# RMSNorm with GELU in fp32: tiles of two rows per partition, statistics in pairs, Gelu in place, and a fixed order of VectorE and ScalarE

## Chip, cores, metric

One core of a Trainium2 chip. The metric is the device time of one execution in us. A kernel's executions spread by at most 0.3%.

## The reference

```python
x: (8, 1024, 2048) float32, gamma: (2048,) float32, eps = 1e-5
rms = np.sqrt(np.mean(x ** 2, axis=-1, keepdims=True) + eps)
out = gamma * x / rms
return 0.5 * out * (1 + np.tanh(np.sqrt(2 / np.pi) * (out + 0.044715 * out ** 3)))
```

8192 rows of 2048 numbers: 67.1 MB in, 67.1 MB out.

## The kernel before

64 tiles of 128 rows. Loads are issued by SyncE, stores by GpSimd. ScalarE squares x with the sum as a by-product (and later does Gelu with the row's factor as its scale); VectorE multiplies by gamma and computes 1/sqrt of the mean square with an integer trick and two Newton steps, nine instructions on one column. A scheduler places the instructions of each engine.

```python
xpool bufs=8; ypool bufs=5; opool bufs=8; spool bufs=12; psum bufs=2
gamma_t = singles.tile([P, D], fp32)
nc.sync.dma_start(out=gamma_t, in_=gamma.partition_broadcast(P))
for i in range(ntiles):                       # 64
    x_t = xpool.tile([P, D], fp32)
    nc.sync.dma_start(out=x_t, in_=x2d[r0:r0 + P, :])
    nc.scalar.activation(out=sq_scratch, in_=x_t, func=Square, scale=inv_d_sqrt, accum_out=ssq)
    y_t = ypool.tile([P, D], fp32)
    nc.vector.tensor_mul(out=y_t, in0=x_t, in1=gamma_t)
    # ... nine VectorE instructions on [P, 1]: rstd from ssq (cut)
    o_t = opool.tile([P, D], fp32)
    nc.scalar.activation(out=o_t, in_=y_t, func=Gelu_apprx_tanh, scale=rstd)
    nc.gpsimd.dma_start(out=out2d[r0:r0 + P, :], in_=o_t)
```

Of the kernel before, what the change touches and what calls it, by code (L numbers as in the profile page):

```python
# [1 line left out]

# [4 lines left out]


@with_exitstack  # L10
def kernel(
    ctx: ExitStack,
    tc: tile.TileContext,
    x: bass.AP,
    gamma: bass.AP,
    eps: bass.AP,
    out: bass.AP,
):
    nc = tc.nc
    P = nc.NUM_PARTITIONS  # L20
    fp32 = mybir.dt.float32

    x2d = x.flatten_outer_dims()
    out2d = out.flatten_outer_dims()
    N, D = x2d.shape
    assert N % P == 0
    ntiles = N // P

    eps_f = float(eps)
    inv_d_sqrt = 1.0 / float(D) ** 0.5  # L30

    MAGIC = 0x5F3759DF

    singles = ctx.enter_context(tc.tile_pool(name="singles", bufs=1))
    xpool = ctx.enter_context(tc.tile_pool(name="xpool", bufs=8))
    ypool = ctx.enter_context(tc.tile_pool(name="ypool", bufs=5))
    opool = ctx.enter_context(tc.tile_pool(name="opool", bufs=8))
    spool = ctx.enter_context(tc.tile_pool(name="spool", bufs=12))
    psum = ctx.enter_context(tc.tile_pool(name="psum", bufs=2, space=bass.MemoryType.PSUM))

    gamma_t = singles.tile([P, D], fp32)
    nc.sync.dma_start(out=gamma_t, in_=gamma.partition_broadcast(P))

    magic_t = singles.tile([P, 1], mybir.dt.int32)
    nc.vector.memset(magic_t, MAGIC)  # L45

    for i in range(ntiles):
        r0 = i * P

        x_t = xpool.tile([P, D], fp32)  # L50
        nc.sync.dma_start(out=x_t, in_=x2d[r0:r0 + P, :])  # L51

        sq_scratch = psum.tile([P, D], fp32)
        stats = spool.tile([P, 8], fp32)
        ssq = stats[:, 0:1]
        nc.scalar.activation(  # L56
            out=sq_scratch,
            in_=x_t,
            func=mybir.ActivationFunctionType.Square,
            scale=inv_d_sqrt,  # L60
            accum_out=ssq,
        )

        y_t = ypool.tile([P, D], fp32)
        nc.vector.tensor_mul(out=y_t, in0=x_t, in1=gamma_t)  # L65

        a = stats[:, 1:2]
        g0 = stats[:, 2:3]
        t0 = stats[:, 3:4]
        t1 = stats[:, 4:5]  # L70
        rstd = stats[:, 5:6]

        nc.vector.tensor_single_scalar(out=a, in_=ssq, scalar=eps_f, op=mybir.AluOpType.add)  # L73
        a_i = a.bitcast(mybir.dt.int32)
        g0_i = g0.bitcast(mybir.dt.int32)
        t0_i = t0.bitcast(mybir.dt.int32)
        nc.vector.tensor_single_scalar(out=t0_i, in_=a_i, scalar=1, op=mybir.AluOpType.arith_shift_right)  # L77
        nc.vector.tensor_tensor(out=g0_i, in0=magic_t, in1=t0_i, op=mybir.AluOpType.subtract)  # L78

        nc.vector.scalar_tensor_tensor(  # L80
            out=t0, in0=g0, scalar=g0, in1=a,
            op0=mybir.AluOpType.mult, op1=mybir.AluOpType.mult,
        )
        nc.vector.tensor_scalar(  # L84
            out=t1, in0=t0, scalar1=-0.5, scalar2=1.5,
            op0=mybir.AluOpType.mult, op1=mybir.AluOpType.add,
        )
        nc.vector.tensor_mul(out=g0, in0=g0, in1=t1)  # L88

        nc.vector.scalar_tensor_tensor(  # L90
            out=t0, in0=g0, scalar=g0, in1=a,
            op0=mybir.AluOpType.mult, op1=mybir.AluOpType.mult,
        )
        nc.vector.tensor_scalar(  # L94
            out=t1, in0=t0, scalar1=-0.5, scalar2=1.5,
            op0=mybir.AluOpType.mult, op1=mybir.AluOpType.add,
        )
        nc.vector.tensor_mul(out=rstd, in0=g0, in1=t1)  # L98

        o_t = opool.tile([P, D], fp32)  # L100
        nc.scalar.activation(  # L101
            out=o_t,
            in_=y_t,
            func=mybir.ActivationFunctionType.Gelu_apprx_tanh,
            scale=rstd,
        )

        nc.gpsimd.dma_start(out=out2d[r0:r0 + P, :], in_=o_t)  # L108


# [1 line left out]
_INS = ['x', 'gamma', 'eps']  # L112
_OUTS = [((8, 1024, 2048), 'float32')]
#: Inputs that are plain numbers.
_NUMBERS = {'eps': 9.999999747378752e-06}


# [26 lines left out]
```

## Time and profile before

| | before |
|---|---|
| time, median of 13 runs | 331.67 us (331.3 to 332.27) |
| span of the profiled run | 330.0 us |
| bytes moved by DMA | 135.35 MB, 410 GB/s over the span |
| VectorE, ScalarE busy | 225.4 us (68%), 247.4 us (75%) |

A page of the profile shows the span in 40 slices of equal length: the busy tenths of each engine, the mean busy share of the 16 DMA engines, and the GB/s that they moved. Here the last two rows say nearly all: from the fourth slice to the 36th the engines' share stands at 9 tenths and the rate at 423 to 429 GB/s, while VectorE is busy for 68% of the span and ScalarE for 75%; in the first three slices and the last four it is lower in places, and there lie the 13.2 us of the span that 135.27 MB at 427 GB/s do not explain. The prediction shows those rows and the windows at both ends. The page lists the packets of one queue as "instruction" (packets, MB, share of the 16 engines' time); they are called fetches below:

```profile
q14 instruction: 9, 0.07, 0.1%
```

### The profile page before, as it was taken

The numbers are of one execution on the slowest core, as the hardware profiler recorded it, in microseconds if no ns is written. First come the engines' busy times: TensorE is split into PE (matmuls) and PEld (weight loads), VectorE is DVE, ScalarE is ACT, GpSimd is POOL, SyncE is SP. The second block draws the span as 40 slices with busy tenths as digits, with TensorE's granted clock in tenths as the row PEclk, the third lists the DMA queues.
The fourth block names the chain that finished last, engine by engine and source line by source line (L and its number), as shares of the span: only waits on it lengthen the run. The fifth ranks groups of instructions, "written<-read, shape, count | busy, mean of one in ns | idle before, by whom it ended". The sixth has DMA issues, their size and how long they took to land.

```text
span 330.0 us, 1300 instructions
## 1 busy us (share of the span) xinstructions
DVE 225.4 (68%) x641; ACT 247.4 (75%) x194; POOL 34.4 (10%) x68
## 2 busy tenths in 40 slices
DVE  0998747647676775958686775949686775869630
ACT  2899794937695969687686969686786969596990
POOL 0020100201010101011010101011010101011110
DMA  8999999999999999999999999999999999999765
GB/s 319 419 382 423 426 426 428 428 428 427 428 427 428 427 426 426 427 429 425 428 427 428 428 427 428 425 426 427 428 427 426 428 427 428 429 427 387 313 286 207
DMA packets 18585, 135.35 MB, mean 410 GB/s; under 512 B 2064, under 2 KB 2064, under 8 KB 2064
## 3 DMA queue, kind: packets, MB, share of 16 engines
q1 hardware_dynamic: 9360, 68.16, 49.2%
q0 software_dynamic: 9216, 67.11, 48.3%
q14 instruction: 9, 0.07, 0.1%
HBM read 68.16 MB, written 67.11 MB: 410 GB/s over the span
## 4 chain that ended last, share of the span: by engine, by line
issue 40%; DMA 40%; ACT 7%; DVE 5%; POOL 5%; POOLq 0%; SPq 0%; ACTq 0%; DVEq 0%
DMA x_t<-in_x_dram 40%; POOL out_dram L108 5%; ACT sq_scratch L56 5%; DVE y_t L65 3%; ACT o_t L101 2%; DVE stats L80 0%; DVE stats L78 0%; DVE stats L77 0%; DVE stats L84 0%; DVE stats L90 0%; POOLq L139 0%; DVE stats L88 0%; DVE stats L73 0%; POOLq L108 0%; SPq L51 0%
## 5 line engine op out<-in xcount | busy, mean ns | idle before, releaser
L65 DVE TENSOR_TENSOR y_t<-x_t,gamma_t 128x2048 f32<-128x2048 f32 x64 | 146.6, 2292 | 76.6 <-DMA x_t<-in_x_dram 73.7
L101 ACT ACTIVATE o_t<-y_t,stats 128x2048 f32<-128x2048 f32 x64 | 123.6, 1991 | 66.2 <-DVE stats L98 66.2
L56 ACT ACTIVATE sq_scratch<-x_t 128x2048 f32<-128x2048 f32 x64 | 119.0, 1859 | 7.0 <-DMA x_t<-in_x_dram 7.0
L108 POOL DMA_DIRECT2D out_dram<-o_t x64 | 34.2, 535 | 287.5 <-ACT o_t L101 287.5
L90 DVE SCALAR_TENSOR_TENSOR stats<-stats 128x1 f32<-128x1 f32 x64 | 13.9, 219 | 1.4
L80 DVE SCALAR_TENSOR_TENSOR stats<-stats 128x1 f32<-128x1 f32 x64 | 13.7, 217 | 1.3
L73 DVE TENSOR_SCALAR stats<-stats 128x1 f32<-128x1 f32 x64 | 9.2, 147 | 5.1 <-ACT sq_scratch L56 5.1
L56 ACT ACTIVATION_READ_ACCUMULATOR sq_scratch<-x_t 128x1 f32 x64 | 11.9, 186 | 0.0
L88 DVE TENSOR_TENSOR stats<-stats 128x1 f32<-128x1 f32 x64 | 10.1, 159 | 1.8
L98 DVE TENSOR_TENSOR stats<-stats 128x1 f32<-128x1 f32 x64 | 10.1, 159 | 1.3
L84 DVE TENSOR_SCALAR stats<-stats 128x1 f32<-128x1 f32 x64 | 9.7, 153 | 1.7
L78 DVE TENSOR_TENSOR stats<-magic_t,stats 128x1 int32<-128x1 int32 x64 | 9.9, 157 | 1.3
L94 DVE TENSOR_SCALAR stats<-stats 128x1 f32<-128x1 f32 x64 | 9.8, 153 | 1.3
L77 DVE TENSOR_SCALAR stats<-stats 128x1 int32<-128x1 int32 x64 | 9.5, 151 | 1.3
L56 ACT ACT_TABLE_LOAD x1 | 1.3, 1283 | 0.7 <-PEq L125 0.7
L101 ACT ACT_TABLE_LOAD x1 | 1.3, 1283 | 0.0
L45 DVE MEMSET magic_t<- 128x1 int32 x1 | 0.1, 59 | 0.8 <-PEq L125 0.8
L125 POOL MEMSET const-float32-0.0<- 128x1 f32 x1 | 0.1, 100 | 0.2 <-issue 0.2
L125 POOL MEMSET const-bfloat16-1.0<- 128x1 bf16 x1 | 0.1, 103 | 0.0
L125 POOL MEMSET const-float32-1.0<- 128x1 f32 x1 | 0.1, 100 | 0.0
L125 POOL MEMSET const-uint8-127<- 128x1 uint8 x1 | 0.1, 100 | 0.0
## 6 DMA issues: line engine op xcount, KB each, us to landing
x_t<-in_x_dram SPq DMA_DIRECT2D x64, 1024.0 KB, 26.2
out_dram<-o_t POOLq DMA_DIRECT2D x64, 1024.0 KB, 12.8
gamma_t<-in_gamma_dram SPq DMA_DIRECT2D x1, 1024.0 KB, 4.5
```

The costliest lines, as they stand in the source:

```text
L56: nc.scalar.activation(out=sq_scratch, in_=x_t, func=mybir.ActivationFunctionType.Square, scale=inv_d_sqrt, accum_out=ssq,)
L65: nc.vector.tensor_mul(out=y_t, in0=x_t, in1=gamma_t)
L77: nc.vector.tensor_single_scalar(out=t0_i, in_=a_i, scalar=1, op=mybir.AluOpType.arith_shift_right)
L78: nc.vector.tensor_tensor(out=g0_i, in0=magic_t, in1=t0_i, op=mybir.AluOpType.subtract)
L80: nc.vector.scalar_tensor_tensor(out=t0, in0=g0, scalar=g0, in1=a, op0=mybir.AluOpType.mult, op1=mybir.AluOpType.mult,)
L84: nc.vector.tensor_scalar(out=t1, in0=t0, scalar1=-0.5, scalar2=1.5, op0=mybir.AluOpType.mult, op1=mybir.AluOpType.add,)
L88: nc.vector.tensor_mul(out=g0, in0=g0, in1=t1)
L90: nc.vector.scalar_tensor_tensor(out=t0, in0=g0, scalar=g0, in1=a, op0=mybir.AluOpType.mult, op1=mybir.AluOpType.mult,)
L94: nc.vector.tensor_scalar(out=t1, in0=t0, scalar1=-0.5, scalar2=1.5, op0=mybir.AluOpType.mult, op1=mybir.AluOpType.add,)
L98: nc.vector.tensor_mul(out=rstd, in0=g0, in1=t1)
L101: nc.scalar.activation(out=o_t, in_=y_t, func=mybir.ActivationFunctionType.Gelu_apprx_tanh, scale=rstd,)
L108: nc.gpsimd.dma_start(out=out2d[r0:r0 + P, :], in_=o_t)
```

## The change

Its intent: fewer and larger transfers with longer contiguous runs, fewer small VectorE instructions, one tile less in SBUF, and an order of the two engines that is fixed by hand.

```diff
+    R = 2                                  # rows per partition in a tile: 32 tiles of 256 rows
+    x3d = x2d.rearrange("(n p r) d -> n p r d", p=P, r=R)
+    o3d = out2d.rearrange("(n p r) d -> n p r d", p=P, r=R)
-    xpool bufs=8, ypool bufs=5, opool bufs=8
+    xpool bufs=5, ypool bufs=5
+    def front(i):
+        x_t = xpool.tile([P, R, D], fp32);  nc.sync.dma_start(out=x_t, in_=x3d[i])
+        for r in range(R):  # Square of x_t[:, r, :], sum to ms[:, r:r + 1]
+        # ... eleven VectorE instructions on [P, R] in place of 2 x nine on [P, 1] (cut)
+        nc.vector.tensor_mul(out=y_t, in0=x_t, in1=gamma_b)       # after the statistics
+        return y_t, g
+    def back(i, y_t, g):
+        for r in range(R):  # Gelu of y_t[:, r, :] in place, scale=g[:, r:r + 1]
+        nc.gpsimd.dma_start(out=o3d[i], in_=y_t)
+    with tc.manual_schedule(engines={DVE, Activation}):
+        prev = front(0)
+        for i in range(1, ntiles):
+            cur = front(i);  back(i - 1, *prev);  prev = cur
+        back(ntiles - 1, *prev)
```

More of the change, by code (lines that the diff above doesn't have):

```diff
@@ L21 @@
     fp32 = mybir.dt.float32
+    int32 = mybir.dt.int32
     x2d = x.flatten_outer_dims()
@@ L25 @@
     N, D = x2d.shape
-    assert N % P == 0
-    ntiles = N // P
+    R = 2
+    rows_per_tile = P * R
+    assert N % rows_per_tile == 0
+    ntiles = N // rows_per_tile
     eps_f = float(eps)
@@ L32 @@
     MAGIC = 0x5F3759DF
+    x3d = x2d.rearrange("(n p r) d -> n p r d", p=P, r=R)
+    o3d = out2d.rearrange("(n p r) d -> n p r d", p=P, r=R)
     singles = ctx.enter_context(tc.tile_pool(name="singles", bufs=1))
-    xpool = ctx.enter_context(tc.tile_pool(name="xpool", bufs=8))
+    xpool = ctx.enter_context(tc.tile_pool(name="xpool", bufs=5))
     ypool = ctx.enter_context(tc.tile_pool(name="ypool", bufs=5))
-    opool = ctx.enter_context(tc.tile_pool(name="opool", bufs=8))
     spool = ctx.enter_context(tc.tile_pool(name="spool", bufs=12))
@@ L39 @@
     psum = ctx.enter_context(tc.tile_pool(name="psum", bufs=2, space=bass.MemoryType.PSUM))
-    gamma_t = singles.tile([P, D], fp32)
+    gamma_t = singles.tile([P, 1, D], fp32)
     nc.sync.dma_start(out=gamma_t, in_=gamma.partition_broadcast(P))
-    magic_t = singles.tile([P, 1], mybir.dt.int32)
+    gamma_b = gamma_t.to_broadcast([P, R, D])
+    magic_t = singles.tile([P, R], int32)
     nc.vector.memset(magic_t, MAGIC)
-    for i in range(ntiles):
-        r0 = i * P
-        x_t = xpool.tile([P, D], fp32)
-        nc.sync.dma_start(out=x_t, in_=x2d[r0:r0 + P, :])
-        sq_scratch = psum.tile([P, D], fp32)
-        stats = spool.tile([P, 8], fp32)
-        ssq = stats[:, 0:1]
-        nc.scalar.activation(
-            out=sq_scratch,
-            in_=x_t,
-            func=mybir.ActivationFunctionType.Square,
-            scale=inv_d_sqrt,
-            accum_out=ssq,
-        )
-        y_t = ypool.tile([P, D], fp32)
-        nc.vector.tensor_mul(out=y_t, in0=x_t, in1=gamma_t)
-        a = stats[:, 1:2]
-        g0 = stats[:, 2:3]
-        t0 = stats[:, 3:4]
-        t1 = stats[:, 4:5]
-        rstd = stats[:, 5:6]
-        nc.vector.tensor_single_scalar(out=a, in_=ssq, scalar=eps_f, op=mybir.AluOpType.add)
-        a_i = a.bitcast(mybir.dt.int32)
-        g0_i = g0.bitcast(mybir.dt.int32)
-        t0_i = t0.bitcast(mybir.dt.int32)
-        nc.vector.tensor_single_scalar(out=t0_i, in_=a_i, scalar=1, op=mybir.AluOpType.arith_shift_right)
-        nc.vector.tensor_tensor(out=g0_i, in0=magic_t, in1=t0_i, op=mybir.AluOpType.subtract)
-        nc.vector.scalar_tensor_tensor(
-            out=t0, in0=g0, scalar=g0, in1=a,
-            op0=mybir.AluOpType.mult, op1=mybir.AluOpType.mult,
-        )
-        nc.vector.tensor_scalar(
-            out=t1, in0=t0, scalar1=-0.5, scalar2=1.5,
-            op0=mybir.AluOpType.mult, op1=mybir.AluOpType.add,
-        )
-        nc.vector.tensor_mul(out=g0, in0=g0, in1=t1)
-        nc.vector.scalar_tensor_tensor(
-            out=t0, in0=g0, scalar=g0, in1=a,
-            op0=mybir.AluOpType.mult, op1=mybir.AluOpType.mult,
-        )
-        nc.vector.tensor_scalar(
-            out=t1, in0=t0, scalar1=-0.5, scalar2=1.5,
-            op0=mybir.AluOpType.mult, op1=mybir.AluOpType.add,
-        )
-        nc.vector.tensor_mul(out=rstd, in0=g0, in1=t1)
-        o_t = opool.tile([P, D], fp32)
-        nc.scalar.activation(
-            out=o_t,
-            in_=y_t,
-            func=mybir.ActivationFunctionType.Gelu_apprx_tanh,
-            scale=rstd,
-        )
-        nc.gpsimd.dma_start(out=out2d[r0:r0 + P, :], in_=o_t)
@@ new lines, in front @@
+    def front(i):
+        x_t = xpool.tile([P, R, D], fp32, name="x_t")
+        nc.sync.dma_start(out=x_t, in_=x3d[i])
+        sq_scratch = psum.tile([P, D], fp32, name="sq_scratch")
+        stats = spool.tile([P, 4, R], fp32, name="stats")
+        ms = stats[:, 0, :]
+        for r in range(R):
+            nc.scalar.activation(
+                out=sq_scratch,
+                in_=x_t[:, r, :],
+                func=mybir.ActivationFunctionType.Square,
+                scale=inv_d_sqrt,
+                accum_out=ms[:, r:r + 1],
+            )
+        a = stats[:, 1, :]
+        g = stats[:, 2, :]
+        t = stats[:, 3, :]
+        nc.vector.tensor_single_scalar(out=a, in_=ms, scalar=eps_f, op=mybir.AluOpType.add)
+        nc.vector.tensor_single_scalar(
+            out=t.bitcast(int32), in_=a.bitcast(int32), scalar=1,
+            op=mybir.AluOpType.arith_shift_right,
+        )
+        nc.vector.tensor_tensor(
+            out=g.bitcast(int32), in0=magic_t, in1=t.bitcast(int32),
+            op=mybir.AluOpType.subtract,
+        )
+        for _ in range(2):
+            nc.vector.tensor_mul(out=t, in0=g, in1=g)
+            nc.vector.tensor_mul(out=t, in0=t, in1=a)
+            nc.vector.tensor_scalar(
+                out=t, in0=t, scalar1=-0.5, scalar2=1.5,
+                op0=mybir.AluOpType.mult, op1=mybir.AluOpType.add,
+            )
+            nc.vector.tensor_mul(out=g, in0=g, in1=t)
+        y_t = ypool.tile([P, R, D], fp32, name="y_t")
+        nc.vector.tensor_mul(out=y_t, in0=x_t, in1=gamma_b)
+        return y_t, g
@@ new lines, in back @@
+    def back(i, y_t, g):
+        for r in range(R):
+            nc.scalar.activation(
+                out=y_t[:, r, :],
+                in_=y_t[:, r, :],
+                func=mybir.ActivationFunctionType.Gelu_apprx_tanh,
+                scale=g[:, r:r + 1],
+            )
+        nc.gpsimd.dma_start(out=o3d[i], in_=y_t)
+    with tc.manual_schedule(engines={mybir.EngineType.DVE, mybir.EngineType.Activation}):
+        prev = front(0)
+        for i in range(1, ntiles):
+            cur = front(i)
+            back(i - 1, *prev)
+            prev = cur
+        back(ntiles - 1, *prev)
```

## The prediction

> **What bounds the kernel now.** I read the page first, from the slices down. The first fence has the busy tenths and the DMA rows of the page before.
>
> ```profile
> DVE  0998747647676775958686775949686775869630
> ACT  2899794937695969687686969686786969596990
> ...
> DMA  8999999999999999999999999999999999999765
> GB/s 319 419 382 423 426 426 428 428 428 427 428 427 428 427 426 426 427 429 425 428 427 428 428 427 428 425 426 427 428 427 426 428 427 428 429 427 387 313 286 207
> ```
>
> From the fourth slice to the 36th the 16 DMA engines are full at 427 GB/s, while VectorE (68% of the span) and ScalarE (75%) have slack. Moving 68.16 MB in and 67.11 MB out at 427 GB/s takes 135.27/0.427 = 316.8 us of the 330.0. So transfers are the bound, and the only time a reordering can win is the other 13.2 us, which lie in the first three slices and the last four. Next the packet counts, then the windows at both ends (columns: window, length, busy time and instruction count of each engine, TensorE clock, DMA share, GB/s).
>
> ```profile
> DMA packets 18585, 135.35 MB, mean 410 GB/s; under 512 B 2064, under 2 KB 2064, under 8 KB 2064
> ```
> ```profile
> 0.00:10.00 10.00, 2.22 (x2) 3.29 (x3) 0.20 (x4) 1.00 0.84 334
> 10.00:20.00 10.00, 9.75 (x32) 8.90 (x7) 0.67 (x1) 1.00 1.00 422
> ...
> 309.00:312.00 3.00, 2.14 (x13) 2.78 (x4) 0.00 (x0) 1.00 0.76 317
> 312.00:315.00 3.00, 0.00 (x0) 3.00 (x2) 1.07 (x2) 1.00 0.66 273
> 315.00:318.00 3.00, 1.91 (x12) 3.00 (x5) 0.00 (x0) 1.00 0.97 393
> 318.00:321.00 3.00, 1.15 (x7) 3.00 (x2) 0.53 (x1) 1.00 0.19 76
> 321.00:324.00 3.00, 0.00 (x0) 0.40 (x1) 0.53 (x1) 1.00 0.98 401
> 324.00:327.00 3.00, 0.00 (x0) 0.00 (x0) 0.00 (x0) 1.00 0.65 265
> 327.00:330.00 3.00, 0.00 (x0) 0.00 (x0) 0.00 (x0) 1.00 0.00 0
> ```
>
> The start loses 10 - 3.34/0.427 = 2.2 us in the first window and 0.1 in the second. The windows 20 to 24 us (328 and 336 GB/s), when the first stores begin, lose 0.9. Together 3.2 us. From 300 us on, 8.6 MB take until 326.3, 26.3 us against 20.1 at full rate, so 6.2 us are holes; then 3.7 us pass with no data. Sum: 316.8 + 3.2 + 6.2 + 3.7 = 329.9, the whole span.
>
> The holes are ScalarE's: it is busy all through 312 to 321 while the DMA idles, because at the end tiles have landed that it has still to process, and a store can't be issued before its Gelu. These are the last instructions (start, duration, engine, line):
>
> ```profile
> 313.64 1.86 ACT L56 ACTIVATE sq_scratch<-x_t 128x2048 f32<-128x2048 f32 x1
> 315.53 1.86 ACT L56 ACTIVATE sq_scratch<-x_t 128x2048 f32<-128x2048 f32 x1
> 317.50 3.89 ACT L101 ACTIVATE o_t<-y_t,stats 128x2048 f32<-128x2048 f32 x2
> 319.80 0.53 POOL L108 DMA_DIRECT2D out_dram<-o_t  x1 [5.24 <-ACT o_t L101]
> 321.69 0.53 POOL L108 DMA_DIRECT2D out_dram<-o_t  x1 [1.36 <-ACT o_t L101]
> ```
>
> The last Square waits for no load: the last load has landed by 305.6 (packet records), 20.6 us before the last byte of a store. The chain of waits, by contrast, calls 40% of the span "issue" and 40% loads; it helps little in a kernel that is bound by queued transfers.
>
> **A quantity to follow: the lead.** Counting packets by queue, the bytes of x loaded less the bytes stored are 7.6 MB when the first store's data starts to flow at 23.3 us. They stay there (7.58 at 60 us, 8.0 at 200, 8.4 at 290)[...]. The lead of the start is thus the backlog of stores at the end, and a larger backlog hides more of the last tiles' computation.
>
> [...]
>
> **The change part by part.**
>
> (1) Tiles of 256 rows, two consecutive rows per partition. The built program has 32 loads and 32 stores of 128x4096, contiguous on both sides, so I expect 16 KB packets: 8,192 instead of 16,384 for x and out, and 1,040 semaphore packets instead of 2,064. [...] I give the saving two chances in three: 2.0 us.
>
> (2) The small VectorE operations: 64 x 9 become 32 x 11, two columns at once. Nine took 1.81 us in a row (315.66 to 317.47), so eleven take about 2.1. [...] VectorE per pair of tiles: 6.5 us. ScalarE: 2 x (1.86+0.19) + 2 x 1.99 less overlaps = 7.8 us. A pair's transfers take 4.19/0.427 = 9.8 us, so both engines keep up in the middle and nothing there ends on the path; VectorE's saving is worth nothing.
>
> (3) Order. The multiplication now stands behind the statistics, and ScalarE does Square(i+1) before Gelu(i). x is freed 3.9 + 0.2 + 2.1 + 4.4 = 10.6 us after landing, against a cycle of 5 x 9.8 = 49 us for its five buffers: some four loads stay queued. The first store is later. The first pair lands at 10.25 (as the second tile did before: the same bytes), Square ends 14.2, statistics 16.5, product 21.0; ScalarE meanwhile does Square of pair 1 and the table load to 20.4, then Gelu to 25.0; issue 25.3. Before, the first issue at 18.70 moved data only from 23.3, 4.6 us later; the same puts it at 29.8. Loads don't run dry: gamma and five pairs are 11.5 MB, worth until 29 us, and the sixth load can be issued at 21.0. So the lead becomes 7.6 + 6.5 x 0.42 = about 10 MB, or 4.8 pairs.
>
> (4) The end. At the last landing T about 10 MB of stores remain instead of some 6.5. Their transfer takes 24 us. The computation after T: Square 3.9 (with start), statistics and product to T+10.8, Gelu (2 x 1.99 less overlap) to T+14.7, issue 0.3, first data 1.0 later (319.80 to 320.7 in the trace): T+16.0. All stores but the last, 8 MB, take until T+18.7. So no hole is left. The 6.2 us of holes go; I keep 0.8 for engines that end unevenly (one engine landed its share of the last load 5 us after the first did; its instruction fetches, nine 8 KB packets before, will be fewer with 840 instead of 1300 instructions).
>
> (5) Gelu in place, without a separate output tile: y is held from its product (landing + 6) to its store's end, 4.8 x 9.8 + 2 = 49 after landing, so 43 of the 49 us that five buffers allow. Just enough; if not, VectorE waits a little behind four queued loads.
>
> Sum: 316.8 + 3.2 + 0.8 + 3.7 = 324.5 span, less 2.0 for the packets = 322.5. The timed run was 1.7 longer than its span: 324.2. For what I overlook I add 1: **325.2 us**.
>
> **Rivals.** (A) *Transfers are the same bytes, so nothing moves*: the last store is twice as large and its computation serial, T+16.0 plus 4.9 us of data, the same as before's 20.6 after the last landing; were the lead still 7.6 MB, T would stay near 305 and the time 331 to 332. For it: the middle is full. Against it: the lead depends on when the first store flows, which the order moves. (B) *A new wait*: y's buffers too tight or ScalarE's fixed order stalling; every pair loses some 0.3 us and the time is 335 to 340. Little speaks for it: both engines have 2 us of slack per pair. (C) *Larger packets help nothing but the holes close*: 326 to 327. (D) *Both gains in full*: 322 to 323.
>
> **Range and chances.** The limit for over 2% is 325.0, inside the gap between C and D. I give A 0.2, B 0.05, the rest to C and D with the packets at two to one. That makes faster 0.48, same 0.48, slower 0.04, and a range of 321.0 to 331.0.
>
> **What would show it.** Right: packets of 16 KB and a middle near 430 GB/s; first store issued near 25 us; the last landing before 301; no window in the last 25 us under 380 GB/s until the data end. Wrong: holes near the end as before (lead not larger), a middle under 425, or VectorE waiting for stores.

The term of 2.0 us for the packets stands as a guess (what was measured of it is under e1). The traces themselves show this: the semaphore packets, as the prediction calls the packets of 4 bytes, took 9 ns each before, and the 8 KB ones 309; and from 60 to 290 us the kernel before loaded 49.5 MB and stored 48.7, so the lead hardly moved.

## The result, and the profile after

| | before | after |
|---|---|---|
| time, median | 331.67 us (13 runs) | 323.62 us (8 runs, 323.25 to 323.87) |
| ratio | | 0.9755, 95% interval 0.9745 to 0.9764 |
| span of the profiled run | 330.0 | 322.0 |
| packets on the DMA engines | 18585 | 9367 |
| VectorE, ScalarE busy | 225.4, 247.4 us | 196.7, 251.4 us |

A ratio is the mean time of one kernel's runs over that of the other's in the same rounds, so not quite the ratio of the medians. The changed kernel is faster by 2.45%. All outputs are right.

The page of the changed kernel: busy tenths, DMA share and rate in 40 slices, the packet counts, and the instruction fetches.

```profile
DVE  0197888887555775546765557765557655567610
ACT  1599999998977778967779777789767798777740
DMA  8999999999999999999999999999999999999994
GB/s 317 429 425 366 433 432 427 431 434 428 433 427 434 431 434 427 432 429 434 429 431 427 438 425 434 427 436 429 432 425 434 434 428 429 436 427 434 428 436 181
DMA packets 9367, 135.32 MB, mean 420 GB/s; under 512 B 1041, under 2 KB 1041, under 8 KB 1041
q14 instruction: 7, 0.05, 0.0%
```

Two things differ from before. The middle runs at about 431 GB/s in place of 427, and the rate holds until the last slice, where before it fell through four slices (387, 313, 286, 207). The dip in the fourth slice (366 GB/s) is the start of the stores, whose first data flow at 30.3 us, as in the third slice before (382 GB/s, first data at 23.3). The windows at both ends (window, length, busy time and count of VectorE, ScalarE and GpSimd, TensorE clock, DMA share, GB/s):

```profile
26.00:28.00 2.00, 1.38 (x1) 1.97 (x3) 0.00 (x0) 1.00 1.08 377
28.00:30.00 2.00, 0.95 (x6) 2.00 (x3) 0.00 (x0) 1.00 1.02 262
...
306.00:310.00 4.00, 0.82 (x1) 3.15 (x2) 0.00 (x0) 1.00 1.00 430
310.00:314.00 4.00, 0.00 (x0) 0.74 (x1) 0.53 (x1) 1.00 1.01 434
314.00:318.00 4.00, 0.00 (x0) 0.00 (x0) 0.00 (x0) 1.00 0.83 356
318.00:322.00 4.00, 0.00 (x0) 0.00 (x0) 0.00 (x0) 1.00 0.02 8
```

Before, ScalarE was busy up to 321 while the DMA engines idled. Now ScalarE is done at 310.7 and the DMA engines still have work until 317 to 320. The last Gelus and the last store (start, duration, engine, line):

```profile
306.85 3.89 ACT L97 ACTIVATE y_t<-y_t,stats 128x2048 f32<-128x2048 f32 x2 [2.78 <-DVE y_t L92]
311.04 0.53 POOL L104 DMA_DIRECT2D out_dram<-y_t  x1 [6.14 <-ACT y_t L97]
```

The last store is issued 10.7 us earlier than before, while the DMA engines still move 434 GB/s (310 to 314 us).

The packet records say more than any view of the page. They hold 16 packets of 4 bytes for each transfer: 2,064 before for 129 transfers, 1,040 after for 65. I read them as one for each of the 16 DMA engines, when that engine's share has landed: those of the last store start between 317.2 and 319.6 us in the changed kernel, and the last of them as the last data packet ends. So one can see how far apart the engines end. The table gives, for all kernels, the rate from 60 to 280 us, the lead (bytes of x loaded less bytes stored, at 200 us), the instruction packets fetched within the span, the landing of the last load and of the last store on the first and on the last of the 16 engines, and the stretch from there to the end of the span. (The page of the changed kernel counts 7 fetches: the seventh is a packet of 32 bytes at 0.07 us.)

| kernel | time us | ratio to before | middle GB/s | lead MB | fetched | last load | last store | stretch |
|---|---|---|---|---|---|---|---|---|
| before | 331.67 | 1 | 426.9 | 8.0 | 9 | 299.1 / 305.3 | 326.0 / 326.2 | 3.8 |
| after | 323.62 | 0.9755 | 431.0 | 10.1 | 6 | 293.5 / 295.9 | 317.2 / 319.6 | 2.5 |
| e1 8 KB rows | 325.63 | 0.9815 | 427.6 | 10.3 | 6 | 294.9 / 297.2 | 319.3 / 321.4 | 2.4 |
| e2 one row | 329.42 | 0.9932 | 426.9 | 6.8 | 10 | 303.6 / 308.0 | 320.8 / 323.6 | 3.8 |
| e3 free order | 337.98 | 1.0185 | 427.3 | 12.6 | 6 | 287.3 / 288.1 | 333.4 / 333.6 | 2.5 |
| e4 three y buffers | 328.48 | 0.9901 | 431.2 | 10.2 | 6 | 293.3 / 295.7 | 323.9 / 324.1 | 2.5 |
| e5 six x buffers | 323.72 | 0.9755 | 431.2 | 10.2 | 6 | 293.4 / 295.6 | 317.1 / 319.3 | 2.5 |
| e6 one row, late Gelu | 329.54 | 0.9932 | 426.9 | 9.6 | 10 | 296.3 / 301.1 | 319.6 / 323.4 | 3.8 |
| e7 gamma by TensorE | 321.34 | 0.9684 | 431.0 | 10.4 | 6 | 290.6 / 293.2 | 314.9 / 316.9 | 2.5 |
| e8 early tiny DMA | 323.80 | 0.9761 | 431.0 | 10.2 | 6 | 293.4 / 295.8 | 317.1 / 319.5 | 2.5 |
| e9 more instructions | 327.79 | 0.9877 | 430.5 | 10.5 | 12 | 292.5 / 299.9 | 321.5 / 323.6 | 2.5 |
| e11 split transfers | 327.84 | 0.9884 | 427.1 | 8.8 | 8 | 299.1 / 301.6 | 319.6 / 322.5 | 3.8 |
| e12 e7 and e8 | 321.55 | 0.9694 | 430.9 | 10.5 | 6 | 290.4 / 292.9 | 314.8 / 317.2 | 2.5 |

### The profile page after: what moved, and what is told of

Same layout as the page of the kernel before. It is cut to its first block, busy times and chain, and to the rows that moved or that the text cites. A ratio compares the mean times of both kernels' runs of the same rounds, so it can differ in the third digit from the quotient of the medians. Undisturbed runs are those within 1.5% of the kernel's fastest.

```text
span 322.0 us, 809 instructions
## 1 busy us (share of the span) xinstructions
DVE 196.7 (61%) x385; ACT 251.4 (78%) x194; POOL 17.4 (5%) x36
## 2 busy tenths in 40 slices
DMA packets 9367, 135.32 MB, mean 420 GB/s; under 512 B 1041, under 2 KB 1041, under 8 KB 1041
## 3 DMA queue, kind: packets, MB, share of 16 engines
q0 software_dynamic: 4608, 67.11, 48.7%
## 4 chain that ended last, share of the span: by engine, by line
DMA 61%; ACT 16%; DVE 13%; issue 6%; POOLq 0%; SPq 0%; ACTq 0%
DMA x_t<-in_x_dram 61%; ACT sq_scratch L61 10%; DVE y_t L92 9%; ACT y_t L97 6%; DVE stats L85 1%; DVE stats L84 1%; DVE stats L83 1%; DVE stats L89 0%; DVE stats L73 0%; DVE stats L72 0%; DVE stats L77 0%; POOLq L143 0%; SPq L47 0%; SPq L55 0%; ACTq L97 0%
## 5 line engine op out<-in xcount | busy, mean ns | idle before, releaser
L61 ACT ACTIVATE sq_scratch<-x_t 128x2048 f32<-128x2048 f32 x64 | 120.3, 1879 | 55.5 <-DMA x_t<-in_x_dram 54.4
L92 DVE TENSOR_TENSOR y_t<-x_t,gamma_t 128x4096 f32<-128x4096 f32 x32 | 141.6, 4424 | 0.0
L97 ACT ACTIVATE y_t<-y_t,stats 128x2048 f32<-128x2048 f32 x64 | 124.1, 1986 | 3.1 <-DVE y_t L92 3.1
L72 DVE TENSOR_SCALAR stats<-stats 128x2 f32<-128x2 f32 x32 | 5.4, 169 | 98.2 <-ACT sq_scratch L61 98.2
L104 POOL DMA_DIRECT2D out_dram<-y_t x32 | 17.2, 537 | 293.9 <-ACT y_t L97 293.9
L85 DVE TENSOR_SCALAR stats<-stats 128x2 f32<-128x2 f32 x64 | 10.9, 170 | 2.2
L84 DVE TENSOR_TENSOR stats<-stats 128x2 f32<-128x2 f32 x64 | 10.3, 161 | 2.2
L83 DVE TENSOR_TENSOR stats<-stats 128x2 f32<-128x2 f32 x64 | 10.3, 161 | 2.2
L89 DVE TENSOR_TENSOR stats<-stats 128x2 f32<-128x2 f32 x64 | 10.3, 161 | 2.2
L73 DVE TENSOR_SCALAR stats<-stats 128x2 int32<-128x2 int32 x32 | 5.4, 170 | 1.1
L77 DVE TENSOR_TENSOR stats<-magic_t,stats 128x2 int32<-128x2 int32 x32 | 5.1, 161 | 1.1
```

What stands on the lines that cost most here:

```text
L61: nc.scalar.activation(out=sq_scratch, in_=x_t[:, r, :], func=mybir.ActivationFunctionType.Square, scale=inv_d_sqrt, accum_out=ms[:, r:r + 1],
L72: nc.vector.tensor_single_scalar(out=a, in_=ms, scalar=eps_f, op=mybir.AluOpType.add)
L73: nc.vector.tensor_single_scalar(out=t.bitcast(int32), in_=a.bitcast(int32), scalar=1, op=mybir.AluOpType.arith_shift_right,)
L77: nc.vector.tensor_tensor(out=g.bitcast(int32), in0=magic_t, in1=t.bitcast(int32), op=mybir.AluOpType.subtract,)
L83: nc.vector.tensor_mul(out=t, in0=g, in1=g)
L84: nc.vector.tensor_mul(out=t, in0=t, in1=a)
```

## The experiments

Each was timed in five rounds beside the kernel before, on the same chip. The lines of the diffs are against the changed kernel.

### e1: the same transfers in 8 KB packets

```diff
-    x3d = x2d.rearrange("(n p r) d -> n p r d", p=P, r=R)
+    x3d = x2d.rearrange("(n r p) d -> n p r d", p=P, r=R)      # o3d likewise
```

> The changed kernel with one thing undone: a partition takes rows p and p+128 of its block, not two neighbouring rows, so the same 2 MB transfers go in 8 KB packets. My theory (a fixed cost per packet): 8 KB packets at 309 ns as before, a middle near 427 GB/s, no holes at the end, 326.6 us, 3 us over the changed kernel. Rival (the cost is per transfer, paid with its semaphore packets, whose number stays halved): the middle stays at 431 GB/s and the time at 323.6 to 324.2 us.

Measured: 325.63 us, 2.0 over the changed kernel. The packet count of the page, and its rates:

```profile
GB/s 312 426 422 382 429 424 432 423 434 424 429 427 426 430 426 431 424 430 428 424 429 427 431 425 432 426 426 428 425 431 426 431 424 430 427 426 431 424 432 200
DMA packets 17558, 135.32 MB, mean 418 GB/s; under 512 B 1040, under 2 KB 1040, under 8 KB 1040
```

The shape is the changed kernel's, full to the last slice, on a lower level. A 16 KB packet takes 611 ns in the changed kernel's records and two of 8 KB take 618 here. 7 ns on 256 packets of each direction and engine are 3.6 us if none of it overlaps; the rates make it 135.27/0.4276 - 135.27/0.4310 = 2.5 us, and the time 2.0. So the same bytes in packets of half the size are shown to take longer, and this is most of the gain in rate. A fixed cost per packet fits; that e1 also hands the rows to the partitions in another order was not tested apart. The rival, a cost per transfer, would have left the time alone; it is not the cause of these 2.0 us.

### e2: the fixed order with tiles of one row

```diff
-    R = 2
+    R = 1
-    xpool bufs=5, ypool bufs=5
+    xpool bufs=8, ypool bufs=10
```

> The changed kernel's fixed order and Gelu in place with tiles of 128 rows (R=1, 8 buffers for x, 10 for y): 1 MB transfers and 8 KB packets as before. Theory L (the larger lead, about 10 MB, is what closed the holes): the first store is issued near 17 us, the lead is some 6.7 MB, smaller than before, the holes stay and the time is 330 us or more. Rival O (the order alone closed them, because ScalarE no longer does Squares in threes while stores wait; after the last landing only about 10 us of computation remain): no holes at the end in spite of the small lead, a middle of 427 GB/s, 326 us.

Measured: 329.42 us, which is neither theory's number. The lead is small, as foreseen (6.8 MB). The windows at the end:

```profile
310.00:314.00 4.00, 3.09 (x12) 2.42 (x3) 0.53 (x1) 1.00 1.02 430
314.00:318.00 4.00, 0.85 (x1) 2.00 (x1) 0.53 (x1) 1.00 0.84 356
318.00:322.00 4.00, 0.00 (x0) 0.00 (x0) 0.00 (x0) 1.00 0.68 283
322.00:326.00 4.00, 0.00 (x0) 0.00 (x0) 0.00 (x0) 1.00 0.03 14
```

The holes are much smaller than before (one is left near 317 us), so the order, with Gelu in place, closes most of them in spite of a smaller lead. Still only 2.3 us are won. The table says why: 13 of the 16 DMA engines are done by 321.0, but one goes on to 323.6 and another to 322.7, and then 3.8 us pass.

### e6: the same with a larger lead

```diff
-            back(i - 1, *prev)
+            back(i - 4, ...)               # against e2; ypool bufs=12
```

> The one-row kernel of e2 with Gelu four tiles behind Square in place of one (12 buffers for y), so that the first store flows some 5 us later and the lead grows from 6.7 to about 9 MB; tile size, packets and instructions are those of e2. Theory L (the lead still costs e2 time): the last landing comes 5 us earlier and the time falls from 329.4 to about 326.5 us. Theory F (e2 is bound by the one engine that also fetches ten packets of instructions, which is never idle): lead up, time the same within 0.7 us of 329.4.

Measured: 329.54 us, the same as e2. The lead rose by 2.8 MB, the last load landed 7 us earlier, and no hole is left, as the slices show (they are full up to the last):

```profile
GB/s 324 420 428 388 427 427 427 429 425 428 429 426 428 429 425 427 430 425 429 428 423 429 429 424 431 425 426 430 427 427 428 427 428 427 427 428 428 425 425 47
```

So the larger lead is worth nothing here, although every wait that I had blamed is gone. Twelve of the engines now end by 319.9; the last one ends at 323.4, where it ended in e2. That is consistent with one engine that is never idle and has more to do than the others. The packet records support it: the landings of the last engine fall behind the median of the 16 in five jumps of 0.6 to 0.75 us, each at one of the ten fetches. (A second engine ends 2.3 us behind; 1.2 of them it loses smoothly from 165 us on, with no jump at a fetch, and that is not explained.)

### e9: more instructions, no more data

```diff
+        junk = jpool.tile([P, 24], fp32, name="junk")
+        for j in range(24):
+            nc.vector.memset(junk[:, j:j + 1], 0.0)      # ahead of the product with gamma
```

> The changed kernel with 24 one-element memsets on VectorE for each pair of tiles (768 more instructions of some 60 ns in VectorE's slack; they write a scratch column that nothing reads). Theory F: the instructions themselves are fetched in 8 KB packets over one of the 16 DMA engines, and that engine ends last and sets the time; 768 instructions are about 6 more such packets, 0.31 us each, so the last store ends 1.9 us later on that engine and at the same time on the others: 325.4 us. Rival (VectorE's slack hides them, the 16 engines end as before): 323.6 us.

Measured: 327.79 us, 4.2 over the changed kernel. The fetches:

```profile
q14 instruction: 12, 0.10, 0.1%
```

Six packets more, as counted (12 against 6); the direction is theory F's and the size is twice it. The last load lands on 15 engines by 294.1 but on one at 299.9 (after: 295.9). The packet records show how. For each load, take how far the last of the 16 landings lies behind their median. This lag is nearly constant, except for jumps, and the jumps come with fetches:

| kernel | fetches after 40 us and before the last load, us | lag of the last engine, us |
|---|---|---|
| after | 42.2, 77.2, 130.4, 228.3, 263.6 | 0.3 at first; 0.8 after 42.2; 1.3 after 130.4; 2.1 after 228.3 |
| e9 | 50.6, 78.0, 80.4, 111.6, 149.4, 181.2, 218.4, 250.9, 266.9, 280.9 | 1.0 at first; eight jumps of 0.65 to 0.95, at all but 78.0 and 266.9; 6.9 at the end |

A jump is longer than the 0.31 us of a fetch because the packet that starts as the fetch ends takes 0.96 to 1.26 us in place of 0.61: at 218.4 us in e9, 0.31 and 0.64 more make the jump of 0.95. Why that packet is slow is not shown. So the fetches do not all fall on one engine, as theory F has it (at 263.6 us in the changed kernel another engine jumps, by 0.54), but the engine that ends last is the one that jumps at most of them: at three of five here, at eight of ten in e9. The last pair's computation waits for it. These are the last pair's first Square, the memsets and the issue of the last store:

```profile
300.35 1.88 ACT L62 ACTIVATE sq_scratch<-x_t 128x2048 f32<-128x2048 f32 x1 [1.90 <-DMA x_t<-in_x_dram]
306.52 0.32 DVE L94 MEMSET junk<- 128x1 f32 x23
315.45 0.53 POOL L109 DMA_DIRECT2D out_dram<-y_t  x1 [6.46 <-ACT y_t L102]
```

In the changed kernel this Square starts at 296.25 and the last store is issued at 311.04. Of the 4.4 us between the two issues 4.1 are thus the late engine, and 0.3 are the memsets' own place on the path. Now the rest of the stores is no longer enough to cover the computation, and a hole opens (343 and 322 GB/s in the slices from 302 us). So e9 shows that fetches delay one engine, and that this delay is nearly all of the 4.2 us.

### e3: pairs without the fixed order

```diff
-    with tc.manual_schedule(...): (front(i), then back(i - 1))
+    for i in range(ntiles):
+        cur = front(i)
+        back(i, *cur)                     # the scheduler places the instructions
```

> The changed kernel without the fixed order: the scheduler places VectorE's and ScalarE's instructions, which it does with up to three pairs of Squares ahead of the Gelus; transfers of 2 MB and packets of 16 KB stay. Theory O (order): the middle is 431 GB/s, but ScalarE has a backlog at the end, holes of some 4 to 7 us come back, 327 to 330 us. Theory L (lead): the first store is as late or later, the lead 10 MB or more, and the time is 323 to 325 us.

Measured: 337.98 us, slower than before by 1.85%. Theory L falls clearly: the lead rises to 12.6 MB, and the time with it. The waits, and the windows of the end:

```profile
DVE y_t L92 <- DMA out_dram<-y_t: 62.6, 16, 7.9
```
```profile
294.00:298.00 4.00, 4.00 (x24) 0.38 (x1) 0.00 (x0) 1.00 0.20 86
298.00:302.00 4.00, 4.00 (x1) 4.00 (x3) 0.20 (x1) 1.00 0.00 0
```

VectorE waited 62.6 us for stores to free y's buffers, which in the changed kernel it never does. The scheduler puts a product ahead of the statistics of tiles that have landed earlier. When that product waits for a store, those statistics wait behind it, ScalarE waits for them, and no new store is issued. Near the end a product starts at 291.10 us after 2.5 us of waiting for a store, the statistics of two pairs follow at 295.44, ScalarE starts its Gelus at 297.62 after 5.3 us idle, and the store after that of 285.04 is issued at 301.81. All stores have drained by 295 and nothing moves for 8 us. With tiles of 2 MB and five buffers the fixed order is thus not a detail but a condition of the gain.

### e4: three buffers for y

```diff
-    ypool bufs=5
+    ypool bufs=3
```

> The changed kernel with 3 buffers for y in place of 5, so that a pair's product has to wait for the store three pairs back: the lead can't be over about 3.4 pairs, 7.1 MB, and everything else, order and packets included, is the same. Theory L: the last landing moves some 6 us later to about 302, a hole comes back before the last store, about 326 to 327 us. Theory O: the middle stays at 431 GB/s, no hole, 323.6 us.

Measured: 328.48 us, 4.9 over the changed kernel. One part of my expectation was wrong: the lead stays at 10.2 MB, and the last load lands when it did, since what doesn't fit in y waits in x. Yet holes come back. The wait that grew, and the windows:

```profile
DVE y_t L92 <- DMA out_dram<-y_t: 88.0, 27, 4.0
```
```profile
302.00:306.00 4.00, 3.68 (x1) 3.97 (x4) 0.53 (x1) 1.00 0.64 268
306.00:310.00 4.00, 2.48 (x12) 4.00 (x4) 0.00 (x0) 1.00 0.79 336
310.00:314.00 4.00, 3.67 (x1) 1.23 (x2) 0.53 (x1) 1.00 0.47 197
```

Through the middle this wait costs nothing (431.2 GB/s). At the end it does: pairs that had landed but were not yet computed gave the DMA engines nothing to move, and the rate fell to 268, 336 and 197 GB/s. With e3 and e6, this settles that the lead as I defined it is the wrong quantity. What they point to is the part of it that is computed and queued as stores, against the computation that is still to be done.

### e11: e1 with its transfers split in two

```diff
-        nc.sync.dma_start(out=x_t, in_=x3d[i])
+        for r in range(R):
+            nc.sync.dma_start(out=x_t[:, r, :], in_=x3d[i][:, r, :])     # the store likewise
```

> The kernel of e1 (pairs in the changed kernel's order, 8 KB packets, 325.6 us) with each 2 MB load and store split into two of 1 MB. Its computation, buffers and order are those of e1; its transfers are those of e2 and e6 (329.5 us), whose instruction count (1420) it does not have (about 870, so 6 or 7 fetched packets in place of 10). Theory F (the fetches on one engine made e2 and e6 slow): under 1 us over e1, 325.8 to 326.6 us. Rival D (the number of transfers made them slow, by their semaphore packets and the 1.3 us longer stretch between the last byte and the end of the span, 3.8 against 2.5 us): 327.5 to 328.5 us, and a last stretch of 3.8 us again.

Measured: 327.84 us, 2.2 over e1. Rival D was right in most of it. The middle differs by only 0.5 GB/s, 0.4 us. The last stretch is 3.8 us again, 1.4 longer than e1's. SyncE's last wait shows it, first e1, then e11 (us in total, times, longest):

```profile
SPq L143 <- PEq L143: 1.4, 2, 0.9
```
```profile
SPq L145 <- PEq L145: 2.7, 2, 2.2
```

All kernels with 64 loads and 64 stores have the long stretch (3.8 us), all with 32 the short one (2.4 to 2.5), whatever their number of instructions (e9 has 1577 and 2.5 us). Why the end of the program takes longer after more transfers, these traces don't say. The remaining 0.4 us or so may belong to two more fetched packets; this was not separated.

### e5, e8: the dip at the start

```diff
-    xpool bufs=5
+    xpool bufs=6                                                  # e5
+    warm_t = singles.tile([P, 8], fp32)
+    nc.gpsimd.dma_start(out=warm_t, in_=x2d[0:P, 0:8])            # e8
```

> The changed kernel with 6 buffers for x in place of 5. The slice at 24 to 32 us moves 366 GB/s, and by 30 us exactly gamma and five loads have moved. If the loads ran dry there for want of a free buffer, a sixth closes the dip: about 1 us less, 322.6 us. If the dip belongs to the start of the first store (load packets take 1.0 to 1.2 us there in place of 0.61[...]), nothing changes: 323.6 us.

> The changed kernel with one tiny DMA (128 x 32 bytes into a scratch tile) issued by GpSimd at the very start. In every run so far the first store's data flows 4.6 to 5.1 us after its issue, against 1.0 us for later stores that find empty queues, and loads run at half speed meanwhile. If that is the first use of GpSimd's queue: the first store flows about 1 us after its issue (26.3 us), the dip moves to the start or goes, the lead falls from 10.2 to about 8.6 MB, and the time is between 322.3 (dip gone) and 324.3 us (a small hole before the last store). If it belongs to the first store itself, nothing changes: 323.6 us, lead 10.2 MB.

Measured: 323.72 and 323.80 us, no change in either. The dip is not a dry queue of loads (e5), nor the first use of GpSimd's queue (e8: first store issued at 25.78, its data at 30.27, 4.5 us later). It belongs to the first store of a run: over all kernels its data appears 4.0 to 5.4 us after its issue (not 4.6 to 5.1, as I had it), and in the 3 us before that the slowest load packets take twice their usual time or more (653 ns in place of 309 before, 1295 in place of 611 after). What it is stays open; e8's DMA was a load, so a first write to memory is not ruled out. It costs 0.9 us before (20 to 24 us) and 1.3 after (26 to 32 us).

### e7, e12: a version that moves fewer bytes

```diff
-    nc.sync.dma_start(out=gamma_t, in_=gamma.partition_broadcast(P))
+    nc.sync.dma_start(out=gamma_1, in_=gamma.partition_broadcast(1))         # 8 KB in place of 1 MB
+    for c in range(0, D, 512):                                               # ones_1: [1, P] of 1.0
+        nc.tensor.matmul(gamma_ps[:, c:c + 512], ones_1, gamma_1[:, c:c + 512], start=True, stop=True)
+    nc.vector.tensor_copy(out=gamma_t[:, 0, :], in_=gamma_ps)                # and xpool bufs=6, psum bufs=1
```

> A version meant to be better: the changed kernel with gamma loaded once (8 KB) and spread over the partitions by TensorE (a column of ones times gamma into PSUM, then a copy by VectorE, which idles there), and 6 buffers for x. If DMA bytes set the time, the 1.05 MB that are no longer moved are worth 1.05/0.431 = 2.4 us: 321.2 us. If something at the start other than bytes sets it (first landing, first store), less than 1 us is won: 322.8 us or more.

> The better version e7 (321.3 us) with the tiny early DMA of e8. If first use is what costs the dip and can be had while the queues are still empty, 0.5 to 1.3 us less: 320.0 to 320.8 us. If not, 321.3 us; if the smaller lead opens a hole, 322 us.

Measured: 321.34 us for e7, 2.3 better than the changed kernel and 3.2% better than the kernel before (ratio 0.9684, interval 0.9671 to 0.9697); 321.55 for e12, so e8's DMA adds nothing. The page of e7:

```profile
DMA packets 9224, 134.28 MB, mean 420 GB/s; under 512 B 1025, under 2 KB 1025, under 8 KB 1025
```

1.04 MB less, worth 2.4 us at 431 GB/s; 2.3 us were measured. Here, where the transfers bind, this saving arrived nearly in full.

## Why the prediction was right, and where its steps were not

The time and the range were right (325.2 us foreseen, 323.6 measured); whether it would be faster by 2% the prediction left open, at 0.48 against 0.48. Step by step:

**What bounds the kernel**: right. Transfers bind, and VectorE's 29 us of saved work lie in its slack. That its saving is worth nothing, step (2), holds for the time and not for the number of instructions: fewer of them are fewer fetches (9 before, 6 after), and in e9, with six more, the last load landed 4.0 us later.

**(1) Packets**: right in kind. The middle rose from 427 to 431 GB/s, worth 135.27/0.4269 - 135.27/0.4310 = 3.0 us, where I had entered 2.0. e1 gives 2.0 us in time to the packets.

**(3) The first store and the lead**: right in numbers. Issue at 25.23 (25.3 foreseen), data at 30.3 (29.8), lead 10.1 MB (10). But the sentence that "a larger backlog hides more of the last tiles' computation" is only half true, as e3, e4 and e6 show.

**(4) The end**: the last landing at 295.9 ("before 301"), the last store issued 15.2 us after it (foreseen 15.0), no hole: right. (The reading of the page before was a little off: its last load landed at 305.3 and not 305.6, 6.2 us after the first engine's share and not 5; a late store's first data came 1.1 us after its issue, not 1.0.) The step that failed is the size of the gain. I entered 6.2 us of holes less 0.8 for uneven engines. What closing the holes is worth by itself is 2.2 us (before to e6). Before, the holes let the engine that is behind catch up: all 16 ended within 0.2 us of each other, at 326.2. Without holes that engine is the bound, and the others end 2.4 us ahead of it in the changed kernel and 3.8 in e6. The term for uneven engines was 0.8 and should have been about 2.2. The prediction named the cause, the fetches, but expected too little of it: three of the six in the changed kernel set the last engine back by 0.65 to 0.74 us each (e9).

**The stretch with no data** was entered as unchanged, 3.7 us, and measured 2.5. This was not foreseen; e11 ties it to the number of transfers.

With the measured terms the sum is: 135.27/0.431 = 313.9 at full rate, 3.5 lost at the start (from the windows, at 431 GB/s), 2.2 until the last engine ends at 319.6, 2.45 after it: 322.05, the measured span of 322.0. The span was thus some 1.5 us shorter than predicted because the packets gave 1.0 more, the last stretch 1.2 more and my reserve of 1 was not needed, against 1.4 that the uneven engines and 0.3 that the start took back. That these nearly cancel is luck.

**(5) In place**: right, VectorE never waits for a store. **Rivals**: A (no gain) and B (a new wait) didn't come true; D, both gains in full, was nearest.

The 8.0 us can be laid out as a staircase of measured kernels, each step one or more parts of the change: 331.7 before; 329.5 with the order, in place and without holes (e6); 327.8 with two rows per tile, so fewer instructions, and still 64 transfers of 1 MB each way in 8 KB packets (e11); 325.6 with half as many transfers (e1); 323.6 with 16 KB packets. Each step is about 2 us. It is one path and not a split into independent parts: without the fixed order the paired kernel loses 14 us (e3), and the step from e6 to e11 changes the grain of the order and the buffers along with the number of instructions. The packet records don't number the engines: the late one is known by its lag alone. That this lag jumps at fetches, by what the fetch and the slow packet after it take, is measured; e9 shows that more instructions make it grow.

## What to carry to other kernels

Where the DMA engines are full, as here at 427 to 431 GB/s, look for time in what surrounds the full stretch, and check the end engine by engine: the average of the 16 hid the one that fell behind, here by 2.4 us (after) to 3.8 (e6), most of it in jumps at fetches of the program. Closing the holes, 6.2 us by my count, won only 2.2 (e6), because this engine was the next bound. At the end it was stores computed and queued that counted, not data landed (e3, e4, e6), so keep an engine from having an instruction that waits for a store ahead of work that stores depend on: in e3 that order cost 14 us. Bytes taken away (gamma's broadcast) arrived nearly in full, 2.3 us of 2.4 (e7); halved counts of packets and of transfers were worth some 2 us each in 325 (e1, e11).
